# Seven block products instead of eight in the first branch projection of an encoder layer

## The chip, the cores and the metric

The kernel runs on one core of one Trainium2 chip. The metric is the device time of one execution in microseconds (us); the median of three executions of the kernel before is 2984.28 us (2983.46 to 2986.47). One further execution was recorded by the hardware profiler, and all rows below are from it.

## What is computed

A bidirectional encoder of DEPTH = 2 layers on two requests (512 and 256 tokens), with a model width of 1024, in fp32. Cut to the stage that matters here, in each layer:

```python
def encoder_layer(x, ...):
    h = rmsnorm(x, norm_mix_g)
    proj = jnp.einsum('bsd,dc->bsc', h, w_in)
    qa, ka, va, qb, kb, vb, rb, glf, glb, ga, gb = jnp.split(proj, ...)
    ya = jnp.einsum('bsc,cd->bsd', mixer_a(qa, ka, va), w_branch_a)
    yb = jnp.einsum('bsc,cd->bsd', mixer_b(qb, kb, vb, rb, ...), w_branch_b)
    merged = jax.nn.sigmoid(ga) * ya + jax.nn.sigmoid(gb) * yb
    x = x + jnp.einsum('bsd,de->bse', merged, w_out)
    h = rmsnorm(x, norm_ffn_g)
    hid = jnp.square(jax.nn.relu(jnp.einsum('bsd,df->bsf', h, w_ff1)))
    return x + jnp.einsum('bsf,fd->bsd', hid, w_ff2)
```

`mixer_a` is a windowed attention whose result has 512 features, `mixer_b` a gated linear attention whose result has 1024. The change is in the product of `mixer_a`'s result with `w_branch_a` (512 x 1024), called the first branch or branch A below.

## The kernel before

Activations lie with features on the 128 partitions and the T = 768 tokens of both requests side by side; a feature tile is 128 x 768. Every fp32 operand is split into a high part, rounded to the type that TensorE multiplies fast (fp32r), and a low part, what the rounding left. A product is three passes: high by high, high by low, low by high (`passes`, L166).

A weight unit (`wunit`, L154) is a raw load on SP's DMA queue into the pool `wraw` of 2 buffers, a cast by ScalarE into `whi`, and a subtraction by VectorE into `wlo` (`sub`, L108); `whi` and `wlo` take two of the 6 buffers of the pool `wsp`. A raw buffer is free again when its `wlo` is made, and a `wsp` buffer when TensorE has used it. `feat_dense` (L244) makes one output tile in two widths, 512 and 256 columns, for the two requests (`feat_tile`, matmul at L224); each accumulates in one of the 3 PSUM buffers of the pool `pac` and is then evicted by a function of the caller, `evac`. Activations lie in two pools of tiles of 128 x 768: `big` (allocated by `b3`, 36 buffers) and `ffp` (by `f3`, 15 buffers).

Products are put into a stream and emitted one after the other, each with the weights of about one unit ahead (`add`, `make_units`, `run_dense`). From this program a scheduler fixes a static order of the instructions for every engine. SP runs its DMA issues in that order too, so an issue that waits for a buffer holds all behind it.

The scheme of seven block products (Strassen, in Winograd's form) is used already for `w_ff2` by `quad_dense` (L332) and for `w_out` by `long_dense` (L368). In `quad_dense` an operand is cut in halves of 384 tokens and paired inner feature tiles (`Quads`, L275, with seven operand blocks B11, B21, B22, T1 to T4 from `first` and `second`), and a weight unit (`wquad`, L309) is loaded by three issues (L313 to L315) into `raw4` and made into seven weight blocks. A block of two output tiles is seven products of 384 columns in three PSUM banks (wA, wB, wC), and each partial sum is handed to a function of the caller, `add_to`.

The stage around the change has, in this order, in each layer: the gate tiles of `ga`, which become `ta` (L1172 to L1186, tiles `sga`); `xa` (L1210), the four operand tiles of branch A, each the sum of two loads from `ma_dram`, by `split_from` (L550, loads at L553, sum at L556, cast L558); gate tiles 0 to 3 of `gb` (`gate_b`, tiles `sgb`, evicted at L547 by VectorE and L548 by ScalarE); branch A's product (L1214 to L1218), whose eviction applies the gate of `ga`; `xb` (L1220), the eight operand tiles of branch B, loaded from `mb_dram`; gate tiles 4 to 7; branch B (L1230 on); and the merge by `w_out`.

Of the kernel before, what the change touches and what calls it, by code (L numbers as in the profile page):

```python
# [14 lines left out]
ALU = mybir.AluOpType  # L15

DM = 1024
# [17 lines left out]
HT = T // 2  # L35
# [41 lines left out]
def encoder(ctx: ExitStack, tc: tile.TileContext, a, y_prompt, y_sample):  # L77
    nc = tc.nc
# [13 lines left out]
    def b3(name, dt=F32, shape=(128, T)):  # L92
        return big.tile(list(shape), dt, tag="b3", name=name)
# [53 lines left out]
    ma_dram = drm.tile([2, 512, T], F32, name="ma_dram")  # L147
# [6 lines left out]
    def wunit(parts, nk, nco):  # L154
        raw = wraw.tile([128, nk, nco], F32, tag="raw", name="raw")
        c = 0
        for src, n in parts:
            nc.sync.dma_start(out=raw[:, :, c:c + n], in_=src.rearrange("(k p) c -> p k c", p=128))
            c += n
        hi = wsp.tile([128, nk, nco], F32R, tag="w", name="whi")  # L160
        lo = wsp.tile([128, nk, nco], F32R, tag="w", name="wlo")
        nc.scalar.copy(hi, raw)  # L162
        sub(lo, raw, hi, side[0])
        return hi, lo
# [63 lines left out]
    def feat_tile(unit, ci, x, t0, n, i, evac):  # L228
        hi, lo = unit
        acc = pac.tile([128, 512], F32, tag="acc", name="acc")  # L230
        c = slice(ci * 128, (ci + 1) * 128)
        ts = slice(t0, t0 + n)
        yield from mm_group(acc, n, len(x), lambda k: [(w[:, k, c], y[:, ts]) for w, y in passes(hi, lo, *x[k])],
                            3 * n / 2400)
        evac(i, t0, n, acc)
        yield 3 * n / 2400
# [3 lines left out]
    def one_later():  # L240
        if later:
            yield from later.popleft()()

    def feat_dense(w, c0, x, evac, ncol=128, splits=SPLITS):  # L244

        nkt = len(x)
        per = 8 // nkt

        def maker(i, m):
            return lambda: wunit([(w[:nkt * 128, c0 + i * 128:c0 + (i + m) * 128], m * 128)], nkt, m * 128)  # L250

        def body(i):
            def f(units):
                for ci in range(per):
                    for t0, n in splits:
                        yield from feat_tile(units[0], ci, x, t0, n, i + ci, evac)
                        yield from one_later()
            return f

        for i in range(0, ncol // 128, per):  # L260
            add([maker(i, per)], body(i))
# [285 lines left out]
        nc.vector.tensor_tensor(out, x, r, op=ALU.mult)  # L547
        return nc.scalar.activation(out, out, AF.Tanh, scale=0.5)  # L548

    def split_from(drams, k, alloc_hi, alloc_lo):  # L550
        xs = [b3("spl") for _ in drams]
        for x, dram in zip(xs, drams):
            nc.sync.dma_start(out=x, in_=dram[k * 128:(k + 1) * 128, :])  # L553
        x = xs[0]
        for y in xs[1:]:
            nc.vector.tensor_tensor(x, x, y, op=ALU.add)  # L556
        hi, lo = alloc_hi("sph", F32R), alloc_lo("spl2", F32R)
        nc.scalar.copy(hi, x)  # L558
        sub(lo, x, hi)
        return hi, lo  # L560
# [498 lines left out]
    for l in range(DEPTH):  # L1059
# [7 lines left out]
        for c0, nco in V_SLICES[4:] + V_SLICES[3::-1] if l == 0 else V_SLICES[::-1]:  # L1067
# [7 lines left out]
            def evac(b, acc, c0=c0, nco=nco, nv=nv):  # L1075
                for t0, n in nm.parts:
                    if t0 <= b * 128 < t0 + n:
                        nm.ready(t0, n)
                t = b3("vst", F32R, (128, 4, 2, 64))
                r = nm.rt[:, b:b + 1]  # L1080
                v = acc[:, 0:256].rearrange("p (h c) -> p h c", h=4)
                nc.scalar.activation(t[:, :, 0], v, AF.Copy, scale=r)
                nc.vector.scalar_tensor_tensor(t[:, :, 1], v, r, t[:, :, 0].bitcast(F32),  # L1083
                                               op0=ALU.mult, op1=ALU.subtract)
                nc.sync.dma_start(out=v_dram[b * 128:(b + 1) * 128, c0 // 64:c0 // 64 + 4], in_=t.bitcast(F32))
                if nv == nco:
                    return
                gl = s1("gl", shape=(128, 32))
                nc.vector.tensor_scalar(gl, acc[:, nv:nco], r, None, op0=ALU.mult)
                gx = s1("gx", F32R, (128, 128))  # L1090
                nc.scalar.copy(gx[:, 0:32], gl)
                sub(gx[:, 32:64], gl, gx[:, 0:32])
                nc.vector.tensor_copy(gx[:, 64:96], gx[:, 0:32].bitcast(F32))
                nc.vector.tensor_copy(gx[:, 96:98], ones[:, 0:2])
                gxs[b] = gx
# [76 lines left out]
        ta = []  # L1172
# [21 lines left out]
        def f3(name, dt=F32, shape=(128, T)):  # L1194
            return ffp.tile(list(shape), dt, tag="f3", name=name)
# [3 lines left out]
        def gate_b(k):  # L1199
# [7 lines left out]

            feat_dense(w_in, C_GB + k * 128, h, evac)

        xa = [split_from((ma_dram[0], ma_dram[1]), k, f3, f3) for k in range(4)]  # L1210
        for k in range(4):
            gate_b(k)

        def evac(k, t0, n, acc):  # L1214
            s = ta[k][:, t0:t0 + n]
            nc.vector.scalar_tensor_tensor(s, s, 1.0, acc[:, :n], op0=ALU.add, op1=ALU.mult)

        feat_dense(a["w_branch_a"][l], 0, xa, evac, ncol=DM)  # L1218
        run_dense()
        xb = [split_from((mb_dram,), k, f3 if k < 7 else b3, b3) for k in range(NK)]  # L1220
        for k in range(4, NK):
# [121 lines left out]
```

## Time and profile before

| | before |
|---|---|
| median of 3 executions | 2984.28 us |
| profiled execution | 2985.19 us |
| its span | 2983.0 us |
| TensorE busy | 2934.7 us, 98% |
| VectorE busy | 2010.6 us, 67% |
| ScalarE busy | 1337.0 us, 45% |
| mean granted TensorE clock | 0.996 |
| DMA moved | 268.27 MB, mean 90 GB/s |

Times are microseconds from the start of the span. PE is TensorE's matmul, DVE is VectorE, ACT is ScalarE, SP is the engine that issues the DMAs, and SPq, in an SP row, is an issue, whose duration includes what it waited for. A matmul row's duration overlaps the next one; the distance of two starts is its pace. A bracket at the end of a row is the time that the engine sat idle before it, and what ended that. Names such as `acc<-hh,whi` are the program's tiles, written and read. A granted clock of 1.00 is 2.4 GHz and of 0.50 is 1.2 GHz.

### The profile page before, as it was taken

What the parts mean: (1) busy time and instruction counts of PE and PEld (TensorE: products, weight loads), DVE (VectorE), ACT (ScalarE), POOL (GpSimd) and SP (SyncE); (2) the same over time, 40 slices, a digit from 0 to 9 for tenths busy, and PEclk for the clock granted to TensorE, in tenths of its full rate; (3) what the DMA queues carried; (4) which work ended last, traced back from release to release, by engine and by line L of the source; (5) the groups of instructions that cost most, each with busy time, mean ns of one, the idle gap of its engine ahead of it and who ended that gap; (6) DMA issues with size and microseconds to landing.
All of it is one profiled execution on the core that took longest, in us unless ns stands there. A gap on an engine that the chain in (4) does not pass through costs nothing.

```text
span 2983.0 us, 48725 instructions
## 1 busy us (share of the span) xinstructions
PE 2934.7 (98%) x18812; PEld 2773.8 (93%) x18812; DVE 2010.6 (67%) x4305; ACT 1337.0 (45%) x2830; POOL 38.3 (1%) x119
## 2 busy tenths in 40 slices
PE   8999999999999999999999999999999999999997
PEld 7988889999889999999999888999988899999997
DVE  5446667676459777776863667677754687777767
ACT  4546665544234433333453566655442253333334
POOL 1000000000000000000000000000000000000000
PEclk9999999999999999999999999999999999999999
DMA  6533332213322222222254333332233232222212
GB/s 206 195 89 86 86 86 78 76 59 93 126 92 87 59 74 66 65 64 72 85 185 149 82 86 86 86 94 74 61 122 101 68 96 62 67 62 73 71 57 71
DMA packets 391575, 268.27 MB, mean 90 GB/s; under 512 B 40720, under 2 KB 364720, under 8 KB 391344
## 3 DMA queue, kind: packets, MB, share of 16 engines
q1 hardware_dynamic: 391344, 265.16, 30.1%
q8 instruction: 149, 2.44, 0.3%
q14 instruction: 82, 0.67, 0.1%
HBM read 217.77 MB, written 47.33 MB: 89 GB/s over the span
## 4 chain that ended last, share of the span: by engine, by line
PE 91%; DVE 4%; DMA 2%; ACT 2%; issue 1%; SPq 0%; POOL 0%; DVEq 0%; ACTq 0%
PE acc L224 64%; PE wA L347 8%; PE wC L347 4%; PE wA L418 2%; PE wB L347 2%; PE op L712 1%; PE go L929 1%; PE pt L700 1%; PE wC L418 1%; PE up L907 1%; PE cp L851 1%; DVE xT L1297 1%; PE ap L889 1%; PE sp L675 1%; PE wB L418 1%
## 5 line engine op out<-in xcount | busy, mean ns | idle before, releaser
L224 PE MATMUL acc<-hh,whi 128*128 128x384 f32 (+2 forms) x2560 | 873.1, 341 | 0.0
L224 PE MATMUL acc<-hl,whi 128*128 128x384 f32 (+2 forms) x2560 | 860.9, 336 | 0.0
L224 PE MATMUL acc<-hh,wlo 128*128 128x384 f32 (+2 forms) x2560 | 859.3, 336 | 0.0
L224 PEld LDWEIGHTS acc<-hh,wlo 128*128 128x128 f32 x2560 | 482.8, 189 | 32.3
L224 PEld LDWEIGHTS acc<-hh,whi 128*128 128x128 f32 x2560 | 483.5, 189 | 26.5
L224 PEld LDWEIGHTS acc<-hl,whi 128*128 128x128 f32 x2560 | 483.8, 189 | 23.3 <-DVE hl L474 0.4
L162 ACT CAST whi<-raw 128x1024 fp32r<-128x1024 f32 (+1 forms) x240 | 252.0, 1050 | 353.2 <-PE acc L224 243.2
L224 PE MATMUL acc<-whi,hh 128*128 128x256 f32 (+1 forms) x1344 | 389.8, 290 | 2.8 <-DVE vst L1083 1.5
L224 PE MATMUL acc<-whi,hl 128*128 128x256 f32 (+1 forms) x1344 | 383.9, 286 | 2.9 <-DVE hl L474 2.8
L224 PE MATMUL acc<-wlo,hh 128*128 128x256 f32 (+1 forms) x1344 | 384.0, 286 | 0.8 <-POOL wlo L108 0.8
L108 DVE TENSOR_TENSOR wlo<-raw,whi 128x1024 fp32r<-128x1024 f32 (+1 forms) x237 | 290.0, 1224 | 75.9 <-ACT whi L162 75.1
L224 PEld LDWEIGHTS acc<-whi,hl 128*128 128x128 f32 x1344 | 259.1, 193 | 4.7 <-DVE hl L474 3.3
L224 PEld LDWEIGHTS acc<-whi,hh 128*128 128x128 f32 x1344 | 258.9, 193 | 4.7 <-issue 2.4
L224 PEld LDWEIGHTS acc<-wlo,hh 128*128 128x128 f32 x1344 | 258.6, 193 | 1.5 <-POOL wlo L108 1.1
L1282 DVE SCALAR_TENSOR_TENSOR rl<-acc,nr 128x384 f32<-128x384 f32 x128 | 71.0, 555 | 186.6 <-PE acc L224 185.3
L1297 DVE TENSOR_TENSOR xT<-xT,wA 128x384 f32<-128x384 f32 x256 | 135.0, 547 | 16.1 <-PE wA L347 15.9
L271 ACT CAST sh<-s 128x512 fp32r<-128x512 f32 x128 | 78.2, 619 | 141.0 <-DVE s L321 82.8
L108 DVE TENSOR_TENSOR ptx<-pt,ptx 128x256 fp32r<-128x256 f32 x192 | 81.2, 423 | 80.9 <-ACT ptx L703 78.5
L1283 ACT ACTIVATE hq<-rl 128x384 f32<-128x384 f32 x128 | 67.1, 524 | 151.6 <-DVE rl L1282 151.6
L224 PE MATMUL acc<-spl,whi 128*128 128x256 f32 (+1 forms) x384 | 129.4, 337 | 0.0
L224 PE MATMUL acc<-sph,whi 128*128 128x256 f32 (+1 forms) x384 | 129.3, 337 | 0.0
L224 PE MATMUL acc<-sph,wlo 128*128 128x256 f32 (+1 forms) x384 | 129.0, 336 | 0.0
(304 smaller groups left out, 5541.7 us busy)
## 6 DMA issues: line engine op xcount, KB each, us to landing
raw<-in_w_in SPq DMA_DIRECT2D x152, 512.0 KB, 3.9
raw<-in_w_ff SPq DMA_DIRECT2D x64, 512.0 KB, 4.1
v_dram<-vst SPq DMA_DIRECT2D x72, 256.0 KB, 2.9
raw<-in_w_ff SPq DMA_DIRECT2D x64, 256.0 KB, 2.9
raw<-in_w_ff SPq DMA_DIRECT2D x128, 128.0 KB, 2.9
v<-v_dram SPq DMA_DIRECT2D x64, 128.0 KB, 4.8
raw<-in_w_branch_b SPq DMA_DIRECT2D x16, 512.0 KB, 4.2
x_dram<-xT SPq DMA_DIRECT2D x16, 384.0 KB, 3.8
```

The source lines that it names most:

```text
L108: eng.tensor_tensor(out, x, hi.bitcast(F32), op=ALU.subtract)
L162: nc.scalar.copy(hi, raw)
L224: nc.tensor.matmul(acc[:, :n], wt, xt, start=(k == 0 and j == 0), stop=(k == nkt - 1 and j == 2))
L271: nc.scalar.copy(hi, x)
L347: nc.tensor.matmul(acc[:, :HT], x, y, start=(new and p == 0 and j == 0), stop=(p == quads.n - 1 and j == 2), skip_group_check=True)
L418: nc.tensor.matmul(acc[:, :HT], x, y, start=(new and p == 0 and j == 0), stop=(p == n - 1 and j == 2), skip_group_check=True)
L675: nc.tensor.matmul(sp[hh][:, (g - 1) * 128:g * 128], q[g][pb, bs], k[g][pb, bs], start=True, stop=True)
L700: nc.tensor.transpose(pt[:, g, hh, :], pr[hh][:, g * 128:(g + 1) * 128], ident)
L712: nc.tensor.matmul(op[:, hh], v[:, hh].rearrange("p s c -> p (s c)"), pT[g][:, hh].rearrange("p s c -> p (s c)"), start=(g == 0), stop=(g ...
L1282: nc.vector.scalar_tensor_tensor(r, acc[:, :n], 0.0, fnorm.r[:, t0:t0 + n], op0=ALU.max, op1=ALU.mult)
L1283: nc.scalar.activation(q[0][:, t0:t0 + n], r, AF.Square)
L1297: nc.vector.tensor_tensor(x, x, acc, op=ALU.add)
```

## The change

Branch A's product goes through `quad_dense` with `Quads(2)`, two pairs of inner feature tiles. Its operands are built by `first` and `second` from the summed loads; for that, `split_from`'s loads and sums become a function of their own, `summed`. The gate of `ga` is applied in `add_a`: of an output block that has two partial sums, the first is copied out of PSUM by ScalarE into a tile `ua`, the second is added to it by VectorE, and the gate follows; a block with a single sum is gated straight from PSUM.

```diff
-    def split_from(drams, k, alloc_hi, alloc_lo):
+    def summed(drams, k):
         xs = [b3("spl") for _ in drams]
         for x, dram in zip(xs, drams):
             nc.sync.dma_start(out=x, in_=dram[k * 128:(k + 1) * 128, :])
         x = xs[0]
         for y in xs[1:]:
             nc.vector.tensor_tensor(x, x, y, op=ALU.add)
+        return x
+
+    def split_from(drams, k, alloc_hi, alloc_lo):
+        x = summed(drams, k)
         hi, lo = alloc_hi("sph", F32R), alloc_lo("spl2", F32R)
         nc.scalar.copy(hi, x)
         sub(lo, x, hi)
...
-        xa = [split_from((ma_dram[0], ma_dram[1]), k, f3, f3) for k in range(4)]
+        qa = Quads(2)
+        for p in range(2):
+            qa.first(p, summed((ma_dram[0], ma_dram[1]), p))
+            qa.second(p, summed((ma_dram[0], ma_dram[1]), p + 2), (f3 if p == 0 else b3,) * 3)
         for k in range(4):
             gate_b(k)
 
-        def evac(k, t0, n, acc):
-            s = ta[k][:, t0:t0 + n]
-            nc.vector.scalar_tensor_tensor(s, s, 1.0, acc[:, :n], op0=ALU.add, op1=ALU.mult)
-
-        feat_dense(a["w_branch_a"][l], 0, xa, evac, ncol=DM)
+        left_a = {}
+
+        def add_a(k, half, acc):
+            s = ta[k][:, half * HT:(half + 1) * HT]
+            if k >= 4 and half == 0:
+                nc.vector.scalar_tensor_tensor(s, s, 1.0, acc, op0=ALU.add, op1=ALU.mult)
+            elif (k, half) not in left_a:
+                left_a[k, half] = f3("ua", shape=(128, HT))
+                nc.scalar.copy(left_a[k, half], acc)
+            else:
+                u = left_a.pop((k, half))
+                nc.vector.tensor_tensor(u, u, acc, op=ALU.add)
+                nc.vector.scalar_tensor_tensor(s, s, 1.0, u, op0=ALU.add, op1=ALU.mult)
+
+        quad_dense(a["w_branch_a"][l], qa, add_a)
         run_dense()
```

In the changed kernel the lines from `split_from` on stand 4 further down, and those behind branch A 17.

The scheduler's order changes with it. In the rows below (line, operation, tile written and tiles read, shape) the number behind a tile's name is that of the buffer use in the program, and the numbers of the two kernels differ.

On SP, in layer 0 ahead of gate tiles 0 to 3, the order before was this; `raw_9476` holds the weights of gate tile 3 and `raw_9537` the first of branch A:

```order
L158 DMA raw_9476<-in_w_in 128x8x128
L553 DMA spl_9312<-ma_dram_90 128x768
L553 DMA spl_9313<-ma_dram_90 128x768
L553 DMA spl_9321<-ma_dram_90 128x768
L553 DMA spl_9322<-ma_dram_90 128x768
L553 DMA spl_9330<-ma_dram_90 128x768
L553 DMA spl_9331<-ma_dram_90 128x768
L553 DMA spl_9339<-ma_dram_90 128x768
L553 DMA spl_9340<-ma_dram_90 128x768
L158 DMA raw_9537<-in_w_branch_a 128x4x256
```

and with the change it is this; `raw_9441` and `raw_9502` hold the weights of gate tiles 2 and 3, and `raw4_9563` is the first weight unit of branch A, in the buffer that `raw_9441` had:

```order
L158 DMA raw_9441<-in_w_in 128x8x128
L158 DMA raw_9502<-in_w_in 128x8x128
L553 DMA spl_9312<-ma_dram_90 128x768
L553 DMA spl_9313<-ma_dram_90 128x768
L313 DMA raw4_9563<-in_w_branch_a 128x4x128
L314 DMA raw4_9563<-in_w_branch_a 128x2x128
L315 DMA raw4_9563<-in_w_branch_a 128x2x128
L553 DMA spl_9321<-ma_dram_90 128x768
L553 DMA spl_9322<-ma_dram_90 128x768
L553 DMA spl_9344<-ma_dram_90 128x768
L553 DMA spl_9345<-ma_dram_90 128x768
L553 DMA spl_9351<-ma_dram_90 128x768
```

The three loads of the first weight unit now stand between the first pair of operand loads and the second.

On VectorE, at the same place, the order before was this, with `sgb_9385` gate tile 0 and `sgb_9446` gate tile 1:

```order
L108 TENSOR_TENSOR wlo_9418<-raw_9415,whi_9417 128x1024
L556 TENSOR_TENSOR spl_9312<-spl_9312,spl_9313 128x768
L556 TENSOR_TENSOR spl_9321<-spl_9321,spl_9322 128x768
L108 TENSOR_TENSOR spl2_9318<-spl_9312,sph_9317 128x768
L108 TENSOR_TENSOR spl2_9327<-spl_9321,sph_9326 128x768
L556 TENSOR_TENSOR spl_9330<-spl_9330,spl_9331 128x768
L108 TENSOR_TENSOR spl2_9336<-spl_9330,sph_9335 128x768
L556 TENSOR_TENSOR spl_9339<-spl_9339,spl_9340 128x768
L108 TENSOR_TENSOR wlo_9479<-raw_9476,whi_9478 128x1024
L108 TENSOR_TENSOR spl2_9345<-spl_9339,sph_9344 128x768
L547 TENSOR_TENSOR sgb_9385<-acc_9360,nr_322 128x512
L547 TENSOR_TENSOR sgb_9385<-acc_9388,nr_322 128x256
```

and with the change it is this, with `sgb_9411` gate tile 0:

```order
L556 TENSOR_TENSOR spl_9321<-spl_9321,spl_9322 128x768
L302 TENSOR_TENSOR t13_9326<-spl_9321,spl_9312 128x384
L304 TENSOR_TENSOR t24_9327<-spl_9321,t13_9326 128x384
L108 TENSOR_TENSOR wlo_9505<-raw_9502,whi_9504 128x1024
L108 TENSOR_TENSOR ql_9331<-spl_9321,qh_9330 128x768
L305 TENSOR_TENSOR t24_9327<-spl_9321,t24_9327 128x384
L108 TENSOR_TENSOR ql_9337<-t13_9326,qh_9336 128x768
L108 TENSOR_TENSOR ql_9341<-t24_9327,qh_9340 128x768
L556 TENSOR_TENSOR spl_9344<-spl_9344,spl_9345 128x768
L547 TENSOR_TENSOR sgb_9411<-acc_9386,nr_322 128x512
```

The eviction of gate tile 0 now stands behind all of the first pair's operand blocks and behind the sum of the next.

On SP, in layer 0 between branch A and branch B, the order before was this; `raw_10077` and `raw_10139` hold the first two weight units of branch B:

```order
L553 DMA spl_9864<-mb_dram_92 128x768
L158 DMA raw_10077<-in_w_branch_b 128x8x128
L553 DMA spl_9870<-mb_dram_92 128x768
L553 DMA spl_9876<-mb_dram_92 128x768
L158 DMA raw_10139<-in_w_branch_b 128x8x128
L553 DMA spl_9882<-mb_dram_92 128x768
L158 DMA raw_10203<-in_w_branch_b 128x8x128
```

and with the change it is this; `raw_10114` holds the weights of gate tile 7, and `raw_10175` and `raw_10237` the first two units of branch B:

```order
L158 DMA raw_10114<-in_w_in 128x8x128
L553 DMA spl_9944<-mb_dram_92 128x768
L553 DMA spl_9950<-mb_dram_92 128x768
L158 DMA raw_10175<-in_w_branch_b 128x8x128
L553 DMA spl_9956<-mb_dram_92 128x768
L158 DMA raw_10237<-in_w_branch_b 128x8x128
L553 DMA spl_9962<-mb_dram_92 128x768
L553 DMA spl_9968<-mb_dram_92 128x768
L553 DMA spl_9974<-mb_dram_92 128x768
L553 DMA spl_9980<-mb_dram_92 128x768
```

Four operand loads of branch B now stand behind the second load of its weights, where before one did.

On VectorE, at the same place, the order before was this; `sgb_9925` is gate tile 4, `sgb_9986` gate tile 5 and `wlo_10019` the low half of gate tile 7's weights:

```order
L108 TENSOR_TENSOR wlo_10019<-raw_10016,whi_10018 128x1024
L547 TENSOR_TENSOR sgb_9925<-acc_9900,nr_322 128x512
L547 TENSOR_TENSOR sgb_9925<-acc_9928,nr_322 128x256
L108 TENSOR_TENSOR spl2_9879<-spl_9876,sph_9878 128x768
L547 TENSOR_TENSOR sgb_9986<-acc_9961,nr_322 128x512
L108 TENSOR_TENSOR spl2_9885<-spl_9882,sph_9884 128x768
L547 TENSOR_TENSOR sgb_9986<-acc_9989,nr_322 128x256
L108 TENSOR_TENSOR wlo_10080<-raw_10077,whi_10079 128x1024
```

and with the change it is this; `sgb_10023` is gate tile 4, `sgb_10084` gate tile 5 and `wlo_10117` the low half of gate tile 7's weights:

```order
L108 TENSOR_TENSOR wlo_10117<-raw_10114,whi_10116 128x1024
L108 TENSOR_TENSOR spl2_9959<-spl_9956,sph_9958 128x768
L108 TENSOR_TENSOR spl2_9965<-spl_9962,sph_9964 128x768
L108 TENSOR_TENSOR spl2_9971<-spl_9968,sph_9970 128x768
L547 TENSOR_TENSOR sgb_10023<-acc_9998,nr_322 128x512
L547 TENSOR_TENSOR sgb_10023<-acc_10026,nr_322 128x256
L108 TENSOR_TENSOR spl2_9977<-spl_9974,sph_9976 128x768
L547 TENSOR_TENSOR sgb_10084<-acc_10059,nr_322 128x512
L108 TENSOR_TENSOR spl2_9983<-spl_9980,sph_9982 128x768
L547 TENSOR_TENSOR sgb_10084<-acc_10087,nr_322 128x256
```

Three operand low halves now stand between that low half and the eviction of gate tile 4, where before none did.

## Rows read from the trace of the kernel before

**Rows 1.** The page, busy time of the engines

```profile
PE 2934.7 (98%) x18812; PEld 2773.8 (93%) x18812; DVE 2010.6 (67%) x4305; ACT 1337.0 (45%) x2830; POOL 38.3 (1%) x119
```

**Rows 2.** The table by stretch (stretch, us, busy by engine, granted clock, DMA), branch A's product

```profile
790.10:823.50 33.40, 33.40 (x194) 29.48 (x193) 15.53 (x23) 6.80 (x8) 0.00 (x0) 1.00 0.30 87
```

**Rows 3.** TensorE's timeline (start, duration), first matmul of branch A's product and first behind it

```profile
790.08 0.40 PE L224 MATMUL acc<-sph,whi 128*128 128x512 f32 x1
...
823.52 0.40 PE L224 MATMUL acc<-hh,whi 128*128 128x512 f32 x1
```

**Rows 4.** TensorE's timeline, eight matmuls of the block products of w_ff2, first and last

```profile
1102.17 0.33 PE L347 MATMUL wC<-ql,sh 128*128 128x384 f32 x1
...
1103.39 0.33 PE L347 MATMUL wA<-qh,sh 128*128 128x384 f32 x1
```

**Rows 5.** The groups by line and shape (ns min/median/max), adds out of PSUM in w_ff2

```profile
L1297 DVE TENSOR_TENSOR xT<-xT,wA x256: 536/546/555, 1028.3 to 2965.6; 128x384 f32<-128x384 f32 x128
```

**Rows 6.** VectorE's timeline, gate tiles 4 to 7

```profile
833.02 1.22 DVE L108 TENSOR_TENSOR wlo<-raw,whi 128x1024 fp32r<-128x1024 f32 x1 [0.34 <-ACT whi L162]
834.17 1.01 DVE L547 TENSOR_TENSOR sgb<-acc,nr 128x512 f32<-128x512 f32 x2
```

**Rows 7.** TensorE's waits in w_ff2 (total us, times, longest)

```profile
PE wA L347 <- DVE xT L1297: 4.7, 5, 1.6
...
PE wC L347 <- ACT sh L271: 2.4, 2, 1.2
PE wC L347 <- DVE xT L1297: 2.0, 6, 0.5
```

**Rows 8.** SP's timeline, ahead of branch A

```profile
742.46 8.72 SPq L158 DMA_DIRECT2D raw<-in_w_in  x2
751.23 4.07 SPq L553 DMA_DIRECT2D spl<-ma_dram  x8
759.18 0.38 SPq L158 DMA_DIRECT2D raw<-in_w_branch_a  x1
```

**Rows 9.** VectorE's timeline, ahead of branch A

```profile
757.92 1.22 DVE L108 TENSOR_TENSOR wlo<-raw,whi 128x1024 fp32r<-128x1024 f32 x1 [0.58 <-ACT whi L162]
759.07 1.82 DVE L556 TENSOR_TENSOR spl<-spl 128x768 f32<-128x768 f32 x2
```

**Rows 10.** SP's timeline, the three loads of a weight unit of w_ff2

```profile
1024.98 0.37 SPq L313 DMA_DIRECT2D raw<-in_w_ff  x1
...
1025.95 0.47 SPq L315 DMA_DIRECT2D raw<-in_w_ff  x1
```

**Rows 11.** SP's timeline, operands of branch B

```profile
826.36 1.05 SPq L553 DMA_DIRECT2D spl<-mb_dram  x2
834.28 0.38 SPq L158 DMA_DIRECT2D raw<-in_w_branch_b  x1
834.70 0.58 SPq L553 DMA_DIRECT2D spl<-mb_dram  x1
```

**Rows 12.** ScalarE's timeline, operands of branch B

```profile
830.86 0.83 ACT L558 CAST sph<-spl 128x768 fp32r<-128x768 f32 x1 [5.48 <-DMA spl<-mb_dram]
...
839.61 0.83 ACT L558 CAST sph<-spl 128x768 fp32r<-128x768 f32 x1 [0.72 <-DMA spl<-mb_dram]
```

**Rows 13.** TensorE's timeline, gate tile 1, narrow half

```profile
770.53 0.28 PE L224 MATMUL acc<-hh,whi 128*128 128x256 f32 x1
```

**Rows 14.** TensorE's timeline, gate tile 5, narrow half

```profile
837.33 0.28 PE L224 MATMUL acc<-hh,whi 128*128 128x256 f32 x1
```

**Rows 15.** The table by stretch, around a fall of the clock in w_ff2

```profile
1475.00:1482.00 7.00, 4.97 (x24) 4.04 (x23) 7.00 (x15) 3.24 (x7) 0.00 (x0) 0.90 0.33 119
1482.00:1485.00 3.00, 3.00 (x14) 3.00 (x13) 1.94 (x5) 1.35 (x3) 0.00 (x0) 0.67 0.64 187
```

**Rows 16.** TensorE's timeline, in that place

```profile
1481.10 0.69 PE L347 MATMUL wA<-qh,sh 128*128 128x384 f32 x1 [1.50 <-DVE xT L1297]
...
1484.09 0.33 PE L347 MATMUL wA<-qh,ah 128*128 128x384 f32 x1
```

## The prediction

> **What bounds the kernel now.** I read the page's busy shares first: TensorE works 2934.7 of 2983.0 us, VectorE 2010.6 [rows 1]. That share is an average, so I went to the stretches the change touches. In the table by stretch the whole first-branch product of layer 0 shows TensorE busy 33.40 of 33.40 us at the full granted clock, and VectorE only 15.53 [rows 2]. TensorE is the limit there, with nothing to win from waits: only fewer or narrower matmuls shorten it, and any new wait costs its full length. Next I read single instructions: TensorE's for the pace, then VectorE's, ScalarE's and the DMA queue's around the two places where the orders shown above differ most, to date each new wait. Layer 1 has the same orders, so I cost one layer, with layer 0's times, and double it.
>
> The profiled execution took 2985.19 us, 0.91 above the median of the runs, 2984.28. I add the sum to the profile's time and give the result on the median's scale. About 0.2% (6 us) is what a measurement of this kernel can tell from no change.
>
> **1. What TensorE saves.** Before, the product runs from 790.08 to 823.52 us: 33.44 us for 192 matmuls (8 output tiles x 2 widths x 4 feature tiles x 3 passes) [rows 3]. After, it is 4 blocks x 7 products x 2 pairs x 3 passes = 168 matmuls of 384 columns. The same code in w_ff2 starts eight such matmuls from 1102.17 to 1103.39, seven steps of 0.174 us [rows 4]; 168 x 0.174 = 29.28. Saving: 4.16 us a layer. It is this small because the seven products act on half of the width and half of each side, and 7/8 is all they give.
>
> **2. Side work inside the product.** A block gives VectorE three adds out of PSUM and four gate steps of 384 columns, about 0.55 us each [rows 5]: 3.9 us. Its weight unit costs sums and low halves of 2816 columns together; by the low half of 1024 columns at 1.22 us [rows 6] I estimate 3.4 us. Together 7.2 us against a block of 7.3 us on TensorE: tight. But the first two weight units are prepared while the gate tiles still run, so inside the product there are about 4 x 3.9 + 2 x 3.4 = 22 us, and 3 or 4 us for the next gates' and operands' low halves, in 29.3. ScalarE gets 12 copies and the casts; before, it had 6.80 busy us there [rows 2]. In w_ff2, 64 such blocks with seven adds each, the waits that show TensorE held by this work sum to 4.7 + 2.4 + 2.0 us [rows 7], or 0.14 us a block. Four blocks: from nothing to 0.6; I take 0.15, one hold of the last block's product. If the cover were gone (all four weight units inside) VectorE would need 28.7 + 3.4 = 32.1 us: 2.8 us over.
>
> **3. First new wait, in the gate tiles ahead of the product.** The rows of the DMA queue above show the three loads of the first Strassen weight unit standing behind the first two operand loads and ahead of the other six. Before, all eight went out one after the other from 751.23, in 4.07 us [rows 8]. The weight's raw buffer comes free only when VectorE has made the low half of gate tile 2, 757.92 + 1.22 = 759.14 [rows 9], and SP issued its next raw load at 759.18 [rows 8]. Three such issues take 1025.95 + 0.47 - 1024.98 = 1.44 us [rows 10], so the second pair leaves from 760.65 on and, at some 4.5 us from issue to use (826.36 to 830.86 for like loads [rows 11, 12]), is there at about 765.1 (764.3 to 766). Ahead of the eviction of gate tile 0, VectorE now has: add, two half-width differences, a weight's low half, an operand's low half, one difference, two low halves, an add: by 0.95, 0.48 and 1.22 us, with the overlap that back-to-back rows show (two of them in 1.82 us [rows 9]), 7 us, with a cast to wait for 0.3 more, then 0.69 for the eviction. It ends near 772.8. TensorE needs that accumulator (it has three) at 770.53 for the narrow half of gate tile 1 [rows 13]. Wait: 2.3 us, between 1.5 and 3.4. Behind it on VectorE stand only the next pair's operands, used 17 us later.
>
> **4. Second new wait, in the gate tiles behind the product.** The operands of branch B now wait for buffers that the Strassen operands hold, so they load late. On SP, four of the eight stand behind the branch-B weight load whose raw buffer is freed by gate tile 7's low half; before, one did. On VectorE three operand low halves now stand ahead of gate tile 4's eviction, two of them of loads behind that raw load. Before: low half at 833.02 + 1.22 = 834.24 [rows 6], raw issued at 834.28, operand at 834.70 [rows 11], cast at 839.61 [rows 12], and the eviction at 834.17 did not wait for it [rows 6]. After, by the same releases: first operand landed 4.5 us behind 834.70, at 839.2; the second, an issue and a transfer later, at about 840.2; cast 0.83, low half 0.95, eviction 0.69: 842.67. TensorE needs that accumulator at 837.33 [rows 14]. Wait: 5.3 us, between 5.0 (second operand right behind the first) and 6.0 (4.9 to land, as the row at 839.61 had). All of branch B's later work then finds its operands ready.
>
> **5. The clock behind these waits.** After an idle of 1.50 us in w_ff2 the granted clock fell: 0.67 in the 3 us behind it [rows 15], that is, 1.2 GHz for most of them, and the nine matmuls from 1481.10 to 1484.09 [rows 16] took 2.99 us where 9 x 0.174 = 1.57 would do. That costs 1.42 us. In the 7 us ahead TensorE had been busy 4.97 [rows 15], so idle 2.0 in all, in pieces. So 5.3 us idle at one go should bring 1.2 GHz for some matmuls: I take 1.5 us (0 to 3, twice the row). 2.3 us idle is about what the row had: I count it half, 0.7 (0 to 1.7). By the Trainium skill ("TensorE: Matmul & The Clock Gate", The HAM clock gate) the lower level belongs to an engine that sat idle, and busy stretches hold the higher. [...]
>
> **Moved, at nothing.** Four w_out loads move into the product from far ahead; they are used a whole branch later and stand on SP behind work already gone. The summed tiles' adds and the operand low halves run beside the gate tiles, where TensorE stays busy until term 3's place.
>
> **The sum**, a layer: -4.16 + 0.15 + 2.3 + 0.7 + 5.3 + 1.5 = +5.8; two: +11.6. The profile's 2985.2 becomes 2996.8, on the median's scale **2996**. With all small ends (1.5, 5.0, clock 0, 0) a layer adds 2.3: 2989. With all large ends (0.6, 3.4, 1.7, 6.0, 3.0): 10.5: 3005.
>
> **Rivals.** *The saving alone (faster).* Buffers come free earlier than I place them, so that the operand pairs arrive before the evictions need them. It decides where the two waits together fall below 4.0 us a layer, for instance when gate 7's low half ends 4 us before 834.2. For it: TensorE now ends the product sooner and the raw loads could run ahead. Against: that low half waits for its cast, the cast for gate 4's weights to be let go by TensorE, so it moves with TensorE, and SP issues in order (one raw pair held it 8.72 us, then eight loads left at once [rows 8]). With no waits: 2984.3 - 8.3 + 0.3 = 2976. "Perfetto Trace Analysis" of the Trainium skill (Identifying the Most-Contended Engine) would have the engine with the highest occupancy optimized first; here that is TensorE, 98%, and by it alone the result is this rival's. Chance 0.11.
> *One wait, no clock (no difference).* The first pair lands in time or the eviction is early; the granted clock holds: -8.3 + 0.3 + 10.6 = +2.6, 2987. Chance 0.14.
> *VectorE becomes the bound of the product.* The 2.8 us of part 2 on top of the forecast: 2 x 2.8, 3002. For it: 7.2 against 7.3 us a block. Against: two units are done ahead. Chance 0.07.
> *It is not what it says*: the order of instructions has 28 groups of six 384-column matmuls a layer where 192 stood, so I give this nothing.
>
> **How the numbers follow.** The forecast's case (both waits, clock between 0 and its upper ends) has 0.68, nearly all of it above 2990.3. With the VectorE rival, slower has 0.75; no difference 0.14; faster 0.11. The range takes in the forecast's case, most of the middle rival and part of the VectorE one: 2985 to 3004, leaving out the faster rival and the ends.
>
> **What would show it.** Right: about 168 matmuls at 0.174 us in the product; one idle of some 2 us ahead of a narrow gate matmul in the gate section, released by VectorE; one of some 5 us in the second gate section, VectorE idle meanwhile waiting for a cast of a branch-B operand; a granted clock below 1.00 behind it; the same in layer 1. Wrong: no TensorE idle over 1 us in those sections (then 2976), or TensorE waiting on adds throughout the product.

## The result, and the profile after

The changed kernel took 3008.92 us (median of five, 3007.47 to 3011.58) against 2984.28: ratio 1.0079, 95% interval 1.0069 to 1.009. That is 24.6 us slower where I had forecast 11.6, and above my range, which ended at 3004. The direction and the places were right; the sizes of two terms were not, and a third part of the loss I had not counted at all. The page after shows TensorE as busy as before:

```profile
PE 2934.1 (98%) x18764; PEld 2777.6 (92%) x18764; DVE 2054.8 (68%) x4401; ACT 1360.6 (45%) x2878; POOL 38.3 (1%) x119
```

TensorE's waits in the profile after (total us, times, longest) have a first line that the kernel before does not have at all:

```profile
PE acc L224 <- DVE sgb L547: 19.4, 4, 6.2
...
PE wA L347 <- DVE xT L1314: 6.2, 7, 1.6
...
PE pt L704 <- ACT t L698: 5.6, 5, 1.6
```

L547 is the eviction of a gate tile. The four waits, on TensorE's timeline (start, duration, idle before it), stand where the prediction put them, at the narrow halves of gate tiles 1 and 5 of each layer [rows 13, 14]:

```profile
775.20 0.39 PE L224 MATMUL acc<-hh,whi 128*128 128x256 f32 x1 [4.00 <-DVE sgb L547]
...
845.04 0.58 PE L224 MATMUL acc<-hh,whi 128*128 128x256 f32 x1 [5.38 <-DVE sgb L547]
...
2254.60 0.58 PE L224 MATMUL acc<-hh,whi 128*128 128x256 f32 x1 [3.77 <-DVE sgb L547]
...
2325.11 0.58 PE L224 MATMUL acc<-hh,whi 128*128 128x256 f32 x1 [6.21 <-DVE sgb L547]
```

Behind each, the table by stretch (start:end, us, busy by engine, granted clock, DMA) shows TensorE busy and its clock down, where the same places before had 1.00:

```profile
775.20:780.20 5.00, 5.00 (x27) 4.91 (x28) 5.00 (x9) 2.41 (x4) 0.00 (x0) 0.66 0.00 0
845.00:850.00 5.00, 4.96 (x27) 4.84 (x28) 3.16 (x5) 2.90 (x5) 0.00 (x0) 0.70 0.00 0
2254.60:2259.60 5.00, 5.00 (x27) 4.89 (x28) 5.00 (x9) 2.46 (x4) 0.00 (x0) 0.69 0.00 0
2325.10:2330.10 5.00, 4.99 (x25) 4.99 (x26) 2.71 (x4) 2.34 (x5) 0.00 (x0) 0.57 0.01 3
```

That is 5.00 x (0.34 + 0.30 + 0.31 + 0.43) = 6.9 us of lost clock, and it stands in TensorE's busy time. The product itself did what it promised. On TensorE's timeline it runs from 796.36 to 824.45, and its last six matmuls, behind the first ones of the next gate tile, from 826.09 to 827.26:

```profile
796.36 0.34 PE L347 MATMUL wA<-b11h,ah 128*128 128x384 f32 x1
...
824.45 0.39 PE L224 MATMUL acc<-hh,whi 128*128 128x512 f32 x1
...
826.09 0.44 PE L347 MATMUL wA<-qh,ah 128*128 128x384 f32 x1
...
827.26 0.39 PE L224 MATMUL acc<-hl,whi 128*128 128x512 f32 x1
```

28.09 + 1.17 = 29.26 us, against 33.44 before [rows 3]. VectorE did not hold it: from 796.40 to 824.40 TensorE was busy 28.00 of 28.00 us and VectorE 21.94.

```profile
796.40:824.40 28.00, 28.00 (x164) 28.00 (x163) 21.94 (x39) 12.87 (x22) 0.00 (x0) 1.00 0.37 107
```

How the first wait came about, on SP's and VectorE's timelines ahead of it (compare [rows 8, 9]):

```profile
760.66 0.47 SPq L315 DMA_DIRECT2D raw<-in_w_branch_a  x1
761.24 3.70 SPq L553 DMA_DIRECT2D spl<-ma_dram  x6
```

```profile
767.33 0.96 DVE L556 TENSOR_TENSOR spl<-spl 128x768 f32<-128x768 f32 x1 [5.20 <-DMA spl<-ma_dram]
...
773.60 0.95 DVE L556 TENSOR_TENSOR spl<-spl 128x768 f32<-128x768 f32 x1
774.47 0.68 DVE L547 TENSOR_TENSOR sgb<-acc,nr 128x512 f32<-128x512 f32 x1
```

VectorE sat idle 5.20 us for the second pair of operand loads, and the eviction that TensorE needed stood behind all that followed. The second wait reads alike, on SP, ScalarE and then VectorE (compare [rows 6, 11]); ScalarE's cast waits for the load, and VectorE's low half for the cast:

```profile
836.49 0.38 SPq L158 DMA_DIRECT2D raw<-in_w_branch_b  x1
836.98 1.94 SPq L553 DMA_DIRECT2D spl<-mb_dram  x4
```

```profile
841.58 2.78 ACT L562 CAST sph<-spl 128x768 fp32r<-128x768 f32 x3 [5.64 <-DMA spl<-mb_dram]
```

```profile
842.45 1.94 DVE L108 TENSOR_TENSOR spl<-spl,sph 128x768 fp32r<-128x768 f32 x2 [5.12 <-ACT sph L562]
844.30 1.01 DVE L547 TENSOR_TENSOR sgb<-acc,nr 128x512 f32<-128x512 f32 x2
```

The span grew by 24.0 us. Waits 19.36, clock 6.9 and the product's 2 x -4.18 make 17.9. Of the other 6.1, 4.8 are small waits elsewhere, most of them in layer 1's attention and w_ff2; the experiments come back to them. The last 1.3 us I cannot assign.

### The profile page after: what moved, and what is told of

Read it like the earlier page. It is cut to its first block, busy times and chain, and to the rows that moved or that the text cites. A ratio compares the mean times of both kernels' runs of the same rounds, so it can differ in the third digit from the quotient of the medians.

```text
span 3007.0 us, 48833 instructions
## 1 busy us (share of the span) xinstructions
PE 2934.1 (98%) x18764; PEld 2777.6 (92%) x18764; DVE 2054.8 (68%) x4401; ACT 1360.6 (45%) x2878; POOL 38.3 (1%) x119
## 3 DMA queue, kind: packets, MB, share of 16 engines
q8 instruction: 148, 2.42, 0.3%
## 4 chain that ended last, share of the span: by engine, by line
PE 87%; DVE 5%; DMA 3%; ACT 2%; issue 1%; SPq 1%; POOL 0%; DVEq 0%; ACTq 0%
PE acc L224 59%; PE wA L347 9%; PE wC L347 4%; PE wA L418 2%; PE wB L347 2%; PE go L933 1%; PE op L716 1%; PE pt L704 1%; PE wC L418 1%; DVE xT L1314 1%; PE up L911 1%; ACT whi L162 1%; PE ap L893 1%; PE cp L855 1%; DVE wlo L108 1%
## 5 line engine op out<-in xcount | busy, mean ns | idle before, releaser
L162 ACT CAST whi<-raw 128x1024 fp32r<-128x1024 f32 (+1 forms) x232 | 243.7, 1050 | 335.3 <-PE acc L224 221.3
L108 DVE TENSOR_TENSOR wlo<-raw,whi 128x1024 fp32r<-128x1024 f32 (+1 forms) x229 | 280.3, 1225 | 79.3 <-ACT whi L162 78.7
L271 ACT CAST sh<-s 128x512 fp32r<-128x512 f32 x144 | 88.1, 620 | 149.4 <-DVE s L321 84.2
L733 DVE TENSOR_TENSOR mt<-mt,op 128x128 f32<-128x128 f32 x288 | 97.0, 351 | 33.0 <-ACT mt L731 28.9
L271 ACT CAST ah<-raw 128x768 fp32r<-128x768 f32 x72 | 60.3, 837 | 130.9 <-PE acc L224 60.7
L108 DVE TENSOR_TENSOR sl<-s,sh 128x512 fp32r<-128x512 f32 x144 | 98.8, 686 | 17.4 <-PE wA L347 10.3
```

What stands on the lines that cost most here:

```text
L108: eng.tensor_tensor(out, x, hi.bitcast(F32), op=ALU.subtract)
L733: nc.vector.tensor_tensor(dst, dst, src, op=ALU.add)
```

## The experiments

Theory A: the whole loss is two waits a layer, made by the order of loads and evictions, and the lower clock behind them; none of it belongs to the seven products. Rival B: the Strassen operands take so many buffers and so much of VectorE that a wait removed in one place comes back in another.

**The first wait removed.** All eight operand loads go out first, and the arithmetic is emitted behind the evictions of gate tiles 0 and 1 (code cut; `loaded` and `added` are the two halves of `summed`; `gate_b` calls `then(k, t0)` behind its eviction).

```diff
-        for p in range(2):
-            qa.first(p, summed((ma_dram[0], ma_dram[1]), p))
-            qa.second(p, summed((ma_dram[0], ma_dram[1]), p + 2), (f3 if p == 0 else b3,) * 3)
+        mas = {k: loaded((ma_dram[0], ma_dram[1]), k) for k in (0, 2, 1, 3)}
+
+        def qa_step(k, t0):
+            if k < 2 and t0 == 0:
+                qa.first(k, added(mas[k]))
+            elif k < 2:
+                qa.second(k, added(mas[k + 2]), (f3 if k == 0 else b3,) * 3)
+
         for k in range(4):
-            gate_b(k)
+            gate_b(k, qa_step)
```

> All eight loads of the first branch's operands are issued ahead of gate tiles 0 to 3, and their sums, differences and low halves are emitted behind the evictions of gate tiles 0 and 1; all else as in the changed kernel. Theory A (the loss is two waits a layer and the lower clock behind each): the first wait goes, 4.00 + 3.77 us in the two layers, and with it the matmuls at 1.2 GHz behind it, some 1.4 us each: 10.5 us less than the changed kernel's 3008.9, about 2998. Rival B (the Strassen operands only move the wait to what is late next, such as the first weight unit): the wait shows up again behind gate tiles 2 or 3 or ahead of the product, and the time stays over 3004.

Measured: 2998.05 us. No wait is left in the first gate section of either layer; of L547 only the second ones remain:

```profile
PE acc L224 <- DVE sgb L547: 11.8, 2, 5.9
```

**The second wait removed.** The same for branch B's operands and gate tiles 4 to 7.

```diff
-        xb = [split_from((mb_dram,), k, f3 if k < 7 else b3, b3) for k in range(NK)]
+        mbs = [loaded((mb_dram,), k) for k in range(NK)]
+        xb = [None] * NK
+
+        def xb_step(g, t0):
+            for k in ({4: (0,), 5: (2,), 6: (4, 5), 7: (7,)} if t0 == 0 else {4: (1,), 5: (3,), 6: (6,), 7: ()})[g]:
+                xb[k] = split_from(None, k, f3 if k < 7 else b3, b3, mbs[k])
+
         for k in range(4, NK):
-            gate_b(k)
+            gate_b(k, xb_step)
```

> The eight operand loads of branch B are issued ahead of gate tiles 4 to 7, and their casts and low halves are emitted behind the evictions of these tiles, two at a time; all else as in the changed kernel. Theory A: the second wait goes, 5.38 + 6.21 us, and some 3.1 us of matmuls at 1.2 GHz: 14.7 us less than 3008.9, about 2994. Rival B: branch B finds its last operands late and waits in their place, some 3 us a layer or more: over 3000.

Measured: 2993.42 us, and the first waits alone remain, 7.5 us in two:

```profile
PE acc L224 <- DVE sgb L547: 7.5, 2, 3.8
```

**Both.** The two edits together.

> Both edits together. Theory A: the gains add, 25 us less than 3008.9: 2984, and if what the two traces leave unexplained (some 7 us of small waits in attention and w_ff2) belongs to the waits' late clock and transfers, down to 2976, which is the kernel before less the 8.3 us that TensorE saves in the product. Rival B: over 2990.

Measured: 2979.99 us, between theory A's two figures, against 2986.49 for the kernel before on the same chip: ratio 0.9977, interval 0.9968 to 0.9986. It beats both kernels. In the table by stretch, the gate section, the product and the next gate section of layer 0 are without a gap and at the full clock:

```profile
760.00:793.40 33.40, 33.40 (x196) 29.87 (x195) 27.93 (x48) 15.87 (x25) 0.00 (x0) 1.00 0.33 106
793.40:822.50 29.10, 29.10 (x167) 28.67 (x166) 22.65 (x41) 11.15 (x20) 0.00 (x0) 1.00 0.60 179
822.50:860.00 37.50, 37.50 (x212) 32.94 (x212) 17.56 (x22) 15.61 (x22) 0.00 (x0) 1.00 0.35 100
```

Rival B falls: no wait came back. Against the kernel before, measured beside each, the changed kernel stands at +24.6 us, the first edit alone at +11.6, the second alone at +6.9 and both at -6.5. So the single edits gave 13.1 and 17.7 us and both together 31.1, which is their sum but for 0.3.

The traces say where this lies. I measure the stage on TensorE's timeline from the last transposes of `mixer_b`'s result, ahead of the gate tiles, to the first matmul of `w_out`. In the kernel before and in the changed kernel, layer 0:

```profile
735.34 0.60 PE L958 MATMUL tp<-eye,o 128*128 128x128 f32 x4
...
923.60 0.34 PE L418 MATMUL wA<-b11h,aop 128*128 128x384 f32 x1
```

```profile
735.85 0.60 PE L962 MATMUL tp<-eye,o 128*128 128x128 f32 x4
...
932.70 0.34 PE L418 MATMUL wA<-b11h,aop 128*128 128x384 f32 x1
```

| us | stage, layer 0 | stage, layer 1 | rest of the span |
|---|---|---|---|
| before | 188.3 | 188.3 | 2606.5 |
| before, second profile | 188.3 | 188.3 | 2607.4 |
| changed | 196.9 | 197.9 | 2612.3 |
| changed, second profile | 199.2 | 198.0 | 2611.4 |
| both edits | 184.1 | 184.1 | 2610.5 |

With both edits the stage is 4.2 us shorter than before in each layer, just what the product saves. So the seven products do pay in full, 8.4 us, once the orders beside them are put right; measured are 6.5, because the rest of the span, in which the change edits nothing, is longer (3 to 4 us in these profiles). It is 2610.0 to 2613.4 us in every profile of the changed kernel and of its variants without padding, whether the waits are there or not.

TensorE is 98% busy in the changed kernel too; the four waits lie in the other 2%, and the lower clock counts as busy time. The Trainium skill's rule to optimize the most-contended engine first ("Perfetto Trace Analysis", Identifying the Most-Contended Engine) gave the sign for the kernel with both edits and the wrong one for the change alone. For TensorE the page goes by the weight loads (93% before [rows 1]) and not by the matmuls, from which the prediction read it; both name the same engine here.

**The clock by itself.** Matmuls that nobody reads fill most of each wait; all else is as in the changed kernel.

```diff
                     for t0, n in splits:
+                        if fill and t0:
+                            spare = pm("fill")
+                            for j in range(fill):
+                                nc.tensor.matmul(spare, units[0][0][:, j % 8], x[j % 8][0][:, 0:512],
+                                                 start=(j == 0), stop=(j == fill - 1))
                         yield from feat_tile(units[0], ci, x, t0, n, i + ci, evac)
...
-            feat_dense(w_in, C_GB + k * 128, h, evac)
+            feat_dense(w_in, C_GB + k * 128, h, evac, fill={1: 14, 5: 20}.get(k, 0))
```

> The changed kernel with matmuls of 512 columns whose result nobody reads, 14 ahead of the narrow half of gate tile 1 and 20 ahead of that of gate tile 5, in each layer: 3.2 and 4.5 us of work at 0.227 us each inside the waits of 4.0, 5.4, 3.8 and 6.2 us. The waits end when they ended; only TensorE is not idle for so long in them. Theory A, its clock part: the granted clock stays at 1.00 behind the waits, and 5.9 us come back: 3003. Rival C (the lower clock there costs nothing, since later waits absorb it, or falls all the same): 3009.

Measured: 3000.78 us, 8.1 less than the changed kernel (10.1 less than its repeat on the same chip, below), with more work on TensorE and the evictions in the order in which they were. The stage of the table above takes 193.6 and 195.2 us, 3.3 and 2.7 less than in the changed kernel's first profile; the other 2 us lie outside it. The table by stretch, right behind the first two waits:

```profile
773.90:778.90 5.00, 5.00 (x33) 4.66 (x34) 5.00 (x10) 3.73 (x6) 0.00 (x0) 1.00 0.00 0
842.10:847.10 5.00, 5.00 (x33) 4.65 (x34) 3.58 (x6) 3.65 (x6) 0.00 (x0) 1.00 0.00 0
```

33 matmuls stand there in 5 us where the changed kernel had 27. So the lower clock is a price of its own, 6 us in the stages of these two profiles, and no later wait absorbs it. Rival C falls. What the Trainium skill says ("TensorE: Matmul & The Clock Gate", The HAM clock gate: the lower level for an idle engine, the higher for a busy one) agrees with these two runs.

**Why the first wait was 4.0 us and not 2.3.** The second pair's loads are held back, so that two loads leave together and not six, and its sum moves out of the eviction's way.

```diff
+        if behind is not None:
+            nc.vector.tensor_copy(xs[0][:, 0:2], behind)
...
-        for p in range(2):
+
+        def qa_pair(p, behind=None):
...
+        qa_pair(0)
         for k in range(4):
-            gate_b(k)
+            gate_b(k, lambda k, t0: qa_pair(1, sgb[0][:, 0:2]) if k == 0 and t0 else None)
```

> The changed kernel with one edit: the four loads of the second pair of the first branch's operands are held back until gate tile 0 is evicted (a two-column copy into the first of them), so that only the two loads that gate tile 0's eviction stands behind leave when the weight unit's three are out; the second pair's sum leaves its place ahead of that eviction. Theory E (my 2.3 us were too small because six loads of 384 KB left together and shared the DMA engines): the sum that waits for the two loads starts some 4.8 us after the first issue, where the changed kernel had 767.33 - 761.24 = 6.1 us, and with the sum's 0.9 us gone too the wait is near 1.7 us in place of 4.0 and 3.8. Rival F (the loads take 6 us there whatever leaves with them, behind the weight unit's three): 6.1 us again, and a wait of some 3 us.

Measured: 3006.17 us; waits of 3.17 and 2.61 us in the first gate sections of layers 0 and 1. SP's and VectorE's timelines:

```profile
759.90 0.88 SPq L555 DMA_DIRECT2D spl<-ma_dram  x2
```

```profile
766.02 0.96 DVE L558 TENSOR_TENSOR spl<-spl 128x768 f32<-128x768 f32 x1 [5.23 <-DMA spl<-ma_dram]
```

From the first issue to the sum it is 766.02 - 759.90 = 6.1 us, as with six loads. My theory E falls, and F stands: what leaves behind the pair does not matter. The wait went down by the sum that was moved, about 1 us. I had taken 4.5 us from a row in which the *first* of two loads was awaited [rows 11, 12]; this sum needs the second. That row's pair in the kernel before, its two issues and their landings:

```profile
L553 SPq DMA_DIRECT2D spl<-mb_dram x2: 424/498/572, 826.4 to 827.0; - x2
DMA to landing us min/median/max: 4.5/4.6/4.8
```

The second load left 0.6 us behind the first and took 4.8, so it was there 5.4 us behind the first issue. At the second place I did count the second load, and there the forecast came within 0.1 us in layer 0. The last 0.7 us of the 6.1, with the weight unit's three loads right ahead, stay open.

**Late loads, or the place of the eviction?** Branch B's loads stay as late as they were, or later; only their casts and low halves are emitted behind the evictions of gate tiles 4 and 5.

```diff
+        def xb_step(g, t0):
+            if g < 6 and t0 == 0:
+                for k in range((g - 4) * 4, (g - 3) * 4):
+                    xb[k] = split_from((mb_dram,), k, f3 if k < 7 else b3, b3)
```

> The changed kernel with branch B's operand loads left as late as they were, or later, among the raw loads of branch B's weights, but with their casts and low halves behind the evictions of gate tiles 4 and 5 on VectorE. Theory G (the second wait's price is the place of the eviction behind late low halves, not the late loads): the second wait goes as it did with early loads, and the time is near the 2993 of that run. Rival H (late loads cost by themselves: branch B or a later eviction waits): 3000 or more.

Measured: 2993.22 us, the same as with early loads, and the second wait is gone in both layers (the two that remain are the first ones):

```profile
PE acc L224 <- DVE sgb L547: 8.0, 2, 4.1
```

Rival H falls. VectorE still waits for a late cast of an operand in that section, but what stands behind it is not needed yet:

```profile
842.09 0.96 DVE L108 TENSOR_TENSOR spl<-spl,sph 128x768 fp32r<-128x768 f32 x1 [1.32 <-ACT sph L562]
```

At this place the price was the eviction's place in VectorE's queue. For the first wait no run separates the two: there the edit that removed it moved the loads too.

**The changed kernel again, and the kernel before again.**

> The changed kernel once more, on this chip. The four waits in the gate sections come back at 3.7 to 6.2 us, and the time is 3009 (by either theory). What differs between its profile and the first one in attention and in w_ff2 is scatter of single executions, and no part of the change.

> The kernel before once more, for its profile: if the small waits in attention (by ScalarE's t) and in w_ff2 (by VectorE's sums) differ here by as much as they do between the first two traces, the 6 us that those traces leave unexplained are scatter; if they are the same as in the first trace, the change reaches them.

Measured: 3010.83 us with four waits of 19.2 us in all, and 2986.06. The waits came back at the same size, but the lower clock behind them cost more, 5.00 x (0.49 + 0.33) + 6.00 x (0.47 + 0.48) = 9.8 us for 6.9:

```profile
774.60:779.60 5.00, 4.92 (x23) 4.92 (x24) 5.00 (x10) 1.89 (x3) 0.00 (x0) 0.51 0.00 0
845.50:851.50 6.00, 6.00 (x27) 5.88 (x28) 3.12 (x5) 2.95 (x5) 0.00 (x0) 0.53 0.00 0
2255.10:2261.10 6.00, 6.00 (x27) 5.86 (x28) 5.02 (x9) 2.54 (x4) 0.00 (x0) 0.52 0.00 0
2325.80:2330.80 5.00, 4.94 (x27) 4.85 (x28) 3.11 (x6) 2.75 (x5) 0.00 (x0) 0.67 0.01 3
```

The attention waits do not repeat exactly. TensorE's waits for ScalarE's `t` in the two profiles of the kernel before, and in the second of the changed kernel, whose first had 5.6 us:

```profile
PE pt L700 <- ACT t L694: 3.0, 5, 1.0
```

```profile
PE pt L700 <- ACT t L694: 4.0, 6, 1.1
```

```profile
PE pt L704 <- ACT t L698: 5.3, 6, 1.9
```

The repeats differ by 1.0 and 0.3 us, the kernels by 1.3 to 2.6. So less than I expected is scatter: with the rest of the span in the table above, most of the other 6 us come with the change, though its edit lies elsewhere. One of these waits has a cause in the traces. A wait near 2712 us, in layer 1's w_ff2, stood in both profiles of the changed kernel and in neither of the kernel before, on TensorE's timeline of the first and of the second:

```profile
2712.13 0.45 PE L347 MATMUL wA<-qh,sh 128*128 128x384 f32 x1 [1.10 <-DVE xT L1314]
```

```profile
2713.01 0.44 PE L347 MATMUL wA<-qh,sh 128*128 128x384 f32 x1 [1.64 <-DVE xT L1314]
```

In the view of DMA between 2702 and 2709 us, a 256 KB load of a weight unit (median us from issue to landing at the end) took 4.4 us, and the queue that brings instructions was active:

```profile
q8 instruction: 1, 0.02, 0.9%
raw<-in_w_ff SPq DMA_DIRECT2D x2, 256.0 KB, 4.4
```

In the kernel before, in the same place (2681 to 2688 us), no instruction fetch is listed and it took 2.8:

```profile
raw<-in_w_ff SPq DMA_DIRECT2D x2, 256.0 KB, 2.8
```

The other runs agree. In the repeat and in the runs with the first, the second and both edits and with the split pair, a fetch began 1.0 to 2.4 us behind the issue of this load; it took 4.2 to 4.9 us, and a wait of 1.1 to 1.7 us stands behind it. In the run with late casts of branch B the fetch began 6.8 us behind the issue; the load took 3.0 us and the wait is missing. In the filled run a fetch fell into another load, near 2506 us, which took 4.2 us, and there a wait of 1.1 us came up.

**The place of the instruction fetches.** 48 tiny matmuls at the start were to put the fetches of TensorE's instructions back where they were; 80 ahead of the kernel before were to bring them to where the change has them. Each of these fp32 matmuls stands as two in the traces (96 and 160), so the fetches moved twice as far, and to other places than meant.

```diff
+    pad = pm("pad")
+    for j in range(48):
+        nc.tensor.matmul(pad[:32, :16], ident[:, 0:32], ones[:, 0:16], start=(j == 0), stop=(j == 47))
```

> The changed kernel with 48 tiny matmuls (16 columns, nobody reads them) at its very start, as many as the change took away in all. TensorE's own instructions come by DMA, 16 KB at a time, one fetch for each 256 or so of its instructions, so their places in the program go back to where they were in layer 1's w_ff2. Theory K (a fetch that falls into the load of a weight unit there makes it late, 4.4 to 4.9 us for 2.9, and the first trace of the changed kernel and its repeat wait for it 1.1 and 1.6 us near 2712): the load takes 2.9 us again and that wait is gone or under 0.4. Rival L (the wait comes from the changed order or buffers): 1.1 to 1.6 us again. The four waits in the gate sections stay.

> The kernel before with 80 such matmuls at its start, which shifts the fetches by the 160 instructions that stand for 96 fewer in a period of 256, that is, to about where the changed kernel has them in layer 1's w_ff2. Theory K: the load there takes 4.4 to 4.9 us, and the wait of 1.1 to 1.6 us that the kernel before does not have shows up in it. Rival L: no such wait.

Measured, changed kernel: no fetch fell into the load, it took 3.0 us, and the wait near 2712 is gone; only the 0.36 us that stood just ahead of it in the changed kernel too is left:

```profile
raw<-in_w_ff SPq DMA_DIRECT2D x1, 256.0 KB, 3.0
```

```profile
2712.61 0.44 PE L347 MATMUL wA<-qh,sh 128*128 128x384 f32 x1 [0.36 <-DVE xT L1317]
```

Theory K holds in this direction, and rival L falls. In the kernel before, the fetch came some 8 us behind the load and missed it, so that run tests nothing there. It took 2999.26 us in its one execution, 16.7 above the one of the kernel before beside it (14.3 between the profiles' spans). Some 6 us are the padding at the start; most of the rest came up in attention, with nothing else of the program changed, and the stage still takes 188.3 us in each layer. The padded changed kernel took 3014.66, so the padding wins nothing by itself.

## Why the prediction was wrong, point by point

The span grew by 24.0 us and I had forecast 11.6. Two terms of the sum were too small, the first wait (3.2 us) and the clock (2.5 us), and the largest part, 6.1 us, was not in the sum. The points in turn:

- **What bounds the kernel, and part 1 (TensorE's saving).** Right: 4.18 us a layer for 4.16.
- **Part 2 (side work).** Right, and a little too dear: nothing for 0.15. The VectorE rival did not come: 21.94 of 28.00 us.
- **Part 3 (first wait).** Right place and cause, wrong size: 4.00 and 3.77 us for 2.3, outside my 1.5 to 3.4. The step that failed is "the second pair leaves from 760.65 on and, at some 4.5 us from issue to use [...], is there at about 765.1": I gave the pair the time of a first load. It was there at 767.33, 6.1 us behind the issue at 761.24. That the issue came 0.6 us later than forecast cost nothing, since TensorE asked for the accumulator 0.7 us later too, at 771.20. The chain from the landing to the eviction's end took 7.8 us; I had used 7.7, though its parts as I listed them make 8.0. This is 3.2 us over both layers.
- **Part 4 (second wait).** Right in layer 0, 5.38 for 5.3; all of it came 2.2 to 2.3 us later than forecast, the weight load's issue (836.49) as well as TensorE's need (839.66), so these shifts cancel. 6.21 in layer 1, a little outside my bounds: the second operand landed 5.8 us behind its issue there, and 5.0 in layer 0. 1.0 us in all. That late loads cause it was only half of it: by the run with late loads the eviction's place is what costs.
- **Part 5 (the clock).** Right in kind, too low: 6.9 us for 4.4, and 9.8 in the repeat. I had counted half of a fall for the shorter waits, 0.7 us; they cost 1.7 and 1.6, and 2.5 and 2.9 in the repeat, as much as the longer ones. The filled waits show that it is the clock.
- **The sum.** These steps make 17.9 us in place of 11.6; the stage in the traces grew by 18.2. The other 6 are a term that the sum does not have: under "Moved, at nothing" it calls the moved loads and sums free, and it leaves the rest of the program at nothing without a reason. The rest of the span was 2606.5 and 2607.4 us before and is 2611.4 and 2612.3 after. One part of it is shown: the change moves the places at which TensorE's instructions are fetched, and where a fetch fell into a load of w_ff2 near 2704 us, the load was late and TensorE waited near 2712. Whether the others, most of them in layer 1's attention, come about in the same way is open; padding alone moves such waits too.
- **The rivals.** "The saving alone" was not this kernel but is the stage with both edits, and of the 8 us that it promised 6.5 were measured. Its condition, the two waits below 4.0 us a layer, was met there with the operands' arithmetic behind the evictions, and at the second place without earlier transfers. "One wait, no clock" did not come: all four waits are there, each with a fall of the clock.

## What to carry to other kernels

Read, for every engine that evicts, what its fixed order puts ahead of the eviction: one instruction there that waits for a load can hold the matmul engine for about as long (VectorE idle 5.2 and 5.1 us, TensorE 4.0 and 5.4), though that engine looks 98% busy. Emit the next stage's arithmetic behind the evictions of the current one; at the second place late loads then did no harm. Price a wait with the clock behind it, and a pair of loads by the second one's landing. And compare the time outside of the changed stage as well: here it grew by 4 to 6 us.

## What the runs showed that I had not expected

- Each wait of 3.8 to 6.2 us cost another 1.5 to 2.9 us at the lower clock, over two profiles. Unread matmuls in the waits held the clock and brought 6 us back in the stage, 8 to 10 in the whole time.
- TensorE's instructions come in fetches of 16 KB: 148 instruction fetches of 2.42 MB in all on the page after, for 2 x 18764 instructions of TensorE, some 254 each if all of them are TensorE's.
- A 256 KB load took 4.2 to 4.9 us in place of 2.7 to 3.1 in seven profiles in which a fetch of instructions began 1.0 to 2.4 us behind its issue. Three such loads in the padded kernel before stayed at 2.9 to 3.0, so it takes more than the coincidence; what, is open.
- 80 tiny matmuls at the start of the kernel before made it 16.7 us slower, in one execution each, of which only some 6 lie at the start.
